# Attention heads taken two at a time: values in both column halves of TensorE's array, scores in both row halves

## Chip, cores and metric

The kernel runs on one core of a Trainium2 chip. The metric is the device time of one execution in microseconds (us). The engines are named as in the profile: PE is TensorE's matmul (PEld its weight loads), DVE is VectorE, ACT is ScalarE, POOL is GpSimd and SP is SyncE. Each engine runs its own queue strictly in order.

## What is computed

256 tokens of width 1024, in float32, pass through two blocks. The first has an HGRN2 mixer, a MoBA attention and a mixture of experts. The second has two layers of FFN, hybrid mixer and FFN. Three attentions matter here. All have 256 queries and 256 keys, so a head's scores are two rows of blocks of 128: 128 queries against 128 keys, and 128 queries against 256 keys.

```python
# MoBA, 8 heads of width 64; one block of 256 keys, so only "own" is left
s_own = einsum('bhqd,bhkd->bhqk', qc, k_own) * scale + rb[:, t5_bucket(dist)]
p = softmax(where(dist >= 0, s_own, -inf));   o = einsum('bhqk,bhkd->bhqd', p, v_own)
# fox, 8 heads of width 64 (in each of two layers)
s_f = einsum('bhqd,bhkd->bhqk', qf, k_f) * scale_f + cf[..., :, None] - cum_f[..., None, :]
p_f = softmax(where(causal, s_f, -inf));      o_f = einsum('bhqk,bhkd->bhqd', p_f, v_f)
# differential, 4 heads with 2 components c of width 64, values of width 128 (two layers)
s_d = einsum('bhcqd,bhckd->bhcqk', qd, k_d) * scale_d
p_d = softmax(where(causal, s_d, -inf));      a_d = p_d[:, :, 0] - lam * p_d[:, :, 1]
o_d = einsum('bhqk,bhkd->bhqd', a_d, v_d)     # then an RMS norm over each head
```

## The kernel before

The whole program is written out by hand: one Python program records the instructions, and the order in which it records them is the order of every engine's queue. No scheduler reorders anything.

**Projections carry the time.** `feat_block` and `tok_block` multiply the 256 tokens by 512 columns of a weight. Numbers are split into a high and a low part, so each product is three matmuls (`mm3`, L295 to L297). After every chunk of 128 rows of the weight the projection calls `fd.tick()`: that is 12 matmuls of 256 columns or 6 of 512. The weights come as raw float32 through a stream of SBUF slots; the **feeder** makes their parts, for 1024 columns at a time (two ticks' worth): ACT copies the high part (L140, buffer `whi`), DVE subtracts to get the low part (L154, `wlo`). `Feeder.fill` issues L140 at the end of every second chunk, just ahead of the tick; the tick runs one step of each background generator and then flushes the waiting L154. So the order on ACT and DVE is: L140 | this tick's step | L154.

**Attention runs in the background.** `moba`, `diff` and `fox` are generators in `fd.bg`; each `yield` ends one tick's step. A head passes through these parts in different ticks: `score` (the matmuls, then on DVE the biased minimum of each block of rows, which also moves the scores out of PSUM, then on ACT the exponential with its sum), `norm` or, in diff, `combine` (DVE: reciprocals, one component minus `lam` times the other), `trans` (three transposes on PE, copied out by ACT as `PT`), and `pv` (values). In `diff` the counter `i` runs over 15 ticks: the score of one component in each of the first 8; `do(3, combine)`, `do(4, trans)`, `do(6, pv)` and `do(8, square)` serve head h at i = first + 2h. After its ticks come the normalisation of the output (`od`, L1706) and, one per tick, two readouts `dx` (four transposes each, copied out by ACT L1717 and DVE L1718). `fox` begins when the diff scores are done and stops after three scores until diff has set `state["diff"]`. `put_heads` (L1782) is the foreground's readout of a projection, four DVE instructions.

**Score operands before.** A head's width is 64, half of the array's 128 rows. Queries of two heads (components) lie one above the other in 128 partitions. The keys, `kp` in MoBA and `kd` in diff, lie in a buffer for each head with the other 64 rows zero, written at the start by `pool.memset`; a score multiplies all 128 rows. fox has padded keys and queries, since two rows of it carry the forget gates.

**Values before.** `pv` of MoBA and fox writes one head's 64 rows of output: its weights are 64 columns wide and use one column half of the array (the trace shows 128*64 as the tile's shape). It does this for one head in a tick.

**PSUM.** Eight banks: four (`pg`) for projections, two (`po`) for the attention's outputs, and two (`pa`) that go round among all the attention's scores (`ms`, `ds`, `fs`), transposes (`mt`, `t3`; the trace calls the latter `t`) and readouts (`dx`). An instruction that takes a `pa` bank waits until the one before in that bank has been read out.

Of the kernel before, what the change touches and what calls it, by code (L numbers as in the profile page):

```python
# [10 lines left out]
F32 = mybir.dt.float32  # L11
# [6 lines left out]
ALU = mybir.AluOpType  # L18
# [162 lines left out]
def body(tc, A, out, taps=None, stop=None):  # L181
# [3 lines left out]
    with es:  # L185
# [12 lines left out]
        def pa(name="a"):  # L198
            return psum.tile([128, 512], F32, tag="a", name=name, bufs=2)
# [258 lines left out]
        def h4(a):  # L458
            return a.rearrange("p (h t) -> p h t", h=4)

        seg = s4[:, 1536:2048]
        pool.memset(seg, 1.0)
# [7 lines left out]
        vm = s6[:, 1024:2048].rearrange("p (t n) -> p t n", t=2)  # L470
        kp = s7.rearrange("p (h s) -> p h s", h=8)
        pool.memset(s7, 0.0)

# [159 lines left out]
        def moba():  # L633
            yield from until("vm")
            Ps, PTk = {}, {}

            def score(h):
                c = h // 2
                s = pa("ms")
                mm(s[:, 0:128], qm[:, c, 0:128], kp[:, h, 0:128], start=True, stop=True)  # L640
                mm(s[:, 128:384], qm[:, c, 128:256], kp[:, h, :], start=True, stop=True)
                P = Pb[h % 4]
                mx = sm(8, "mx")
                dve.tensor_tensor_reduce(P[:, 0:128], s[:, 0:128], TB[:, h, 128:256], 1.0, 3e38, ALU.add, ALU.min,
                                         mx[:, 2:3])
                dve.tensor_tensor_reduce(P[:, 128:384], s[:, 128:384], TB[:, h, :], 1.0, 3e38, ALU.add, ALU.min,
                                         mx[:, 3:4])
                act(P[:, 0:128], P[:, 0:128], AF.Exp, bias=mx[:, 2:3], scale=-1.0, accum_out=mx[:, 4:5])
                act(P[:, 128:384], P[:, 128:384], AF.Exp, bias=mx[:, 3:4], scale=-1.0, accum_out=mx[:, 5:6])
                Ps[h] = P, mx  # L650

# [14 lines left out]

            def pv(h):
                PT = PTk.pop(h)
                c, e = divmod(h, 2)
                o = oT[c // 2][64 * e:64 * e + 64, (c % 2) * 256:(c % 2) * 256 + 256]  # L670
                mm(o, vm[:, 0, h * 64:h * 64 + 64], PT[:, 0:256], start=c % 2 == 0, stop=False, skip_group_check=True)
                mm(o[:, 128:256], vm[:, 1, h * 64:h * 64 + 64], PT[:, 256:384], start=False, stop=c % 2 == 1,
                   skip_group_check=True)

            for i in range(8 + 4):
                if i == 4:
                    oT = [po("mo") for _ in range(2)]
                if i >= 4:
                    pv(i - 4)
                if 2 <= i < 10:  # L680
                    trans(i - 2)
                if 1 <= i < 9:
                    norm(i - 1)
# [31 lines left out]
        for c in range(4):  # L715
            z = halfbank(banks, c)
            act(kp[0:64, 2 * c], z[0:64], AF.Identity, bias=bcol[0:64, 20 + c:21 + c])
            act(kp[64:128, 2 * c + 1], z[64:128], AF.Identity, bias=bcol[64:128, 20 + c:21 + c])
        banks = tok_block()
# [814 lines left out]
        def mixer(l, g_next):  # L1534
            s_qf, s_kf, s_kd, s_d, s_f, s_p = [st.take() for _ in range(6)]
            qf = s_qf.rearrange("p (h t) -> p h t", h=8)
            kf = s_kf.rearrange("p (h t) -> p h t", h=8)
            kd = s_kd.rearrange("p (h t) -> p h t", h=8)
            qd = s_d[:, 0:1024].rearrange("p (h t) -> p h t", h=4)
# [13 lines left out]
            for a in (OH, OL):  # L1553
                pool.memset(a[:, 0:4].bitcast(F32), 0.0)
            for a in (s_kd, s_qf, s_kf):
                pool.memset(a, 0.0)
# [67 lines left out]
            def put_k(b, x2, r2):  # L1624
                for c in range(2):
                    pr_ = slice(64 * c, 64 * c + 64)
                    dve.tensor_tensor(kd[pr_, 4 * b + c:4 * b + 4:2], x2[pr_], r2[pr_], ALU.add)

# [3 lines left out]
            def trans3(P, i):  # L1632
                p = pa("t3")
                for j in range(3):
                    nc.tensor.transpose(p[:, j * 128:(j + 1) * 128], P[:, j * 128:(j + 1) * 128], ident)  # L1635
                PT = PTs[i % 2] if i >= 0 else work.tile([128, 384], F32, name="PT")
                act(PT, p[:, 0:384], AF.Copy)
                return PT

            def diff():  # L1640
# [3 lines left out]

                def score(n):
                    h, c = divmod(n, 2)
                    s = pa("ds")
                    mm(s[:, 0:128], qd[:, h, 0:128], kd[:, n, 0:128], start=True, stop=True)
                    mm(s[:, 128:384], qd[:, h, 128:256], kd[:, n, :], start=True, stop=True)
                    P = PD[n % 5]  # L1650
                    if c == 0:
                        mxs[h] = sm(16, "md")
                    mx = mxs[h]
                    soft(s, P, mx[:, 2 * c:], mx[:, 8 + 2 * c:])
                    Ps[n] = P

# [32 lines left out]
                def trans(h):  # L1689
                    PTk[h] = trans3(Ps[2 * h], h)  # L1690


                for i in range(15):
                    do(6, pv)
                    do(4, trans)
                    do(3, combine)
                    do(8, square)
                    if i < 8:
                        score(i)
                    if i == 7:  # L1700
                        state["diff scores"] = True
                    yield
# [20 lines left out]
            def fox():  # L1723
# [17 lines left out]

                def pv(h):
                    PT = PTk.pop(h)
                    c, e_ = divmod(h, 2)
                    o = oT[c // 2][64 * e_:64 * e_ + 64, (c % 2) * 256:(c % 2) * 256 + 256]
                    mm(o, vf[:, 0, h * 64:h * 64 + 64], PT[:, 0:256], start=c % 2 == 0, stop=False,  # L1746
                       skip_group_check=True)
                    mm(o[:, 128:256], vf[:, 1, h * 64:h * 64 + 64], PT[:, 256:384], start=False, stop=c % 2 == 1,
                       skip_group_check=True)

                def out_(b):
# [4 lines left out]
                while i < 8 + 4:  # L1756
                    if i >= 3 and not {"diff", "vf"} <= state.keys():
                        yield
                        continue
                    if i >= 4:  # L1760
                        oT = oT or [po("fo") for _ in range(2)]
                        pv(i - 4)
# [164 lines left out]
```

## Time and profile before

| | us |
|---|---|
| three runs | 1678.40, 1681.79, 1682.06 (median 1681.79) |
| profiled execution, its own time | 1678.18 |
| its span, first to last instruction | 1676.4 |
| mean granted clock of TensorE | 0.975 of full speed |
| busy: PE / DVE / ACT | 1544.8 / 813.4 / 650.2 |

MoBA stands at about 110 to 143 us, the differential heads and fox of the first layer at about 919 to 983 us; the second layer repeats them later. The times in the rows are the profiler's, counted from the span's start. A busy time of one instruction holds its fill and drain, so successive instructions of one engine overlap in the rows; what one costs in a queue is read from start to start.

### The profile page before, as it was taken

The page shows a single profiled execution, that of the slowest core. Times are in us where ns is not written, and L with a number is a line of the kernel's source. Part 1 is how long each engine was busy: PE and PEld are TensorE (multiplying, and loading weights), DVE is VectorE, ACT ScalarE, POOL GpSimd, SP SyncE. Part 2 cuts the span into 40 slices and gives each one's busy share as a digit, 9 for nine tenths or more (in the row PEclk, how much of TensorE's full clock was granted, in tenths as well). Part 3 has the DMA queues.
Part 4 walks back from the last instruction along what each step waited for, and adds up shares of the span by engine and source line. Part 5 has one row for each costly group of instructions (what it writes and reads, how often), then busy time and mean ns, then how long its engine had stood idle before and what let it go on. Part 6 is the DMA issues. An engine that isn't in the chain of part 4 may idle for free.

```text
span 1676.4 us, 24622 instructions
## 1 busy us (share of the span) xinstructions
PE 1544.8 (92%) x10204; PEld 1209.8 (72%) x10204; DVE 813.4 (49%) x1215; ACT 650.2 (39%) x964; POOL 99.8 (6%) x144
## 2 busy tenths in 40 slices
PE   8999997877687776899999999999999999999998
PEld 7889972222122221699989879999999989889997
DVE  5875650000000000855567866555655568665554
ACT  6456420000000100644445654444544455654442
POOL 4010020000000100100002000000000030000000
PEclk9999999989998898999999999999999999999999
DMA  9657679999999999875614545555555524465510
GB/s 351 172 182 284 259 300 422 421 421 421 421 421 421 419 421 392 350 270 179 198 38 160 215 193 201 197 189 193 189 199 186 169 65 151 176 254 186 194 58 26
DMA packets 85989, 417.53 MB, mean 249 GB/s; under 512 B 7432, under 2 KB 7640, under 8 KB 50544
## 3 DMA queue, kind: packets, MB, share of 16 engines
q1 hardware_dynamic: 82688, 407.07, 64.1%
q0 software_dynamic: 2912, 7.79, 1.6%
q8 instruction: 82, 1.34, 0.3%
q10 hardware_dynamic: 272, 1.05, 0.2%
q14 instruction: 35, 0.29, 0.0%
HBM read 414.60 MB, written 1.25 MB: 248 GB/s over the span
## 4 chain that ended last, share of the span: by engine, by line
PE 56%; DVE 4%; ACT 1%; issue 0%; POOLq 0%; DVEq 0%; POOL 0%; ACTq 0%
PE g L297 9%; PE g L296 8%; PE g L295 8%; PE o L297 5%; PE o L295 5%; PE o L296 5%; PE a L296 3%; PE a L295 3%; PE a L297 3%; DVE wlo L154 1%; PE tp L1368 1%; PE ey L1105 0%; PE fo L1746 0%; PE t L1635 0%; DVE slot L1782 0%
## 5 line engine op out<-in xcount | busy, mean ns | idle before, releaser
L154 DVE TENSOR_TENSOR wlo<-slot,whi 128x1024 fp32r<-128x1024 f32 x268 | 323.3, 1223 | 196.7 <-ACT whi L140 196.5
L140 ACT ACTIVATE whi<-slot 128x1024 fp32r<-128x1024 f32 x268 | 278.3, 1057 | 217.3 <-PE o L296 67.6
L295 PE MATMUL o<-XH,whi 128*128 128x256 f32 x640 | 177.5, 277 | 0.0
L296 PE MATMUL o<-XL,whi 128*128 128x256 f32 x640 | 177.2, 277 | 0.0
L297 PE MATMUL o<-XH,wlo 128*128 128x256 f32 x640 | 177.2, 277 | 0.0
L295 PE MATMUL g<-whi,OH 128*128 128x512 f32 x416 | 165.5, 398 | 0.0
L297 PE MATMUL g<-whi,OL 128*128 128x512 f32 x416 | 164.0, 394 | 0.0
L296 PE MATMUL g<-wlo,OH 128*128 128x512 f32 x416 | 163.1, 392 | 0.0
L295 PE MATMUL a<-XH,whi 128*128 128x256 f32 x512 | 141.8, 277 | 0.0
L296 PE MATMUL a<-XL,whi 128*128 128x256 f32 x512 | 141.7, 277 | 0.0
L297 PE MATMUL a<-XH,wlo 128*128 128x256 f32 x512 | 141.6, 277 | 0.0
L1087 DVE TENSOR_TENSOR eb<-eb,eu 128x512 f32<-128x512 f32 x8 | 5.5, 687 | 265.5 <-PE eu L1083 255.8
L296 PEld LDWEIGHTS o<-XL,whi 128*128 128x128 f32 x640 | 120.4, 188 | 0.7
L295 PEld LDWEIGHTS o<-XH,whi 128*128 128x128 f32 x640 | 120.2, 188 | 0.7
L297 PEld LDWEIGHTS o<-XH,wlo 128*128 128x128 f32 x640 | 120.2, 188 | 0.0
L295 PE MATMUL g<-XH,whi 128*128 128x256 f32 x384 | 114.2, 297 | 0.0
L296 PE MATMUL g<-XL,whi 128*128 128x256 f32 x384 | 107.0, 279 | 0.0
L297 PE MATMUL g<-XH,wlo 128*128 128x256 f32 x384 | 107.0, 279 | 0.0
L1086 ACT ACTIVATE eb<-eg 128x512 f32<-128x512 f32 x8 | 4.8, 597 | 241.7 <-PE eu L1083 191.8
L296 PEld LDWEIGHTS a<-XL,whi 128*128 128x128 f32 x512 | 96.2, 188 | 0.7
L295 PEld LDWEIGHTS a<-XH,whi 128*128 128x128 f32 x512 | 96.1, 188 | 0.7
L297 PEld LDWEIGHTS a<-XH,wlo 128*128 128x128 f32 x512 | 96.2, 188 | 0.0
(531 smaller groups left out, 3486.8 us busy)
## 6 DMA issues: line engine op xcount, KB each, us to landing
slot<-in_gu_dram SPq DMA_DIRECT2D x71, 1024.0 KB, 4.9
slot<-in_w_gate_up_dram SPq DMA_DIRECT2D x46, 1024.0 KB, 19.8
slot<-in_w_in_dram SPq DMA_DIRECT2D x35, 1024.0 KB, 5.1
slot<-in_dn_dram SPq DMA_DIRECT2D x35, 1024.0 KB, 4.9
ew<-in_w_gate_up_dram SPq DMA_DIRECT2D x31, 1024.0 KB, 19.8
slot<-in_w_down_dram SPq DMA_DIRECT2D x29, 1024.0 KB, 19.8
e<-in_w_gate_up_dram SPq DMA_DIRECT2D x15, 1024.0 KB, 19.8
ew<-in_w_down_dram SPq DMA_DIRECT2D x14, 1024.0 KB, 19.8
```

The costliest lines, as they stand in the source:

```text
L140: self.nc.scalar.activation(hi[:, c], src[:, c], AF.Copy)
L154: self.low.tensor_tensor(lo[:, c], src[:, c], hi.bitcast(F32)[:, c], ALU.subtract)
L295: mm(o, sh, mh, start=start, stop=False, skip_group_check=skip)
L296: mm(o, sh, ml, start=False, stop=False, skip_group_check=skip)
L297: mm(o, sl, mh, start=False, stop=stop, skip_group_check=skip)
L1086: act(esg, g, AF.Silu)
L1087: dve.tensor_tensor(esg, esg, u, ALU.mult)
L1368: nc.tensor.transpose(p[:, i * 128:(i + 1) * 128], src[:, c], ident)
```

## The change

Three things are done.

1. **Values in pairs.** A new helper `weighted` takes the values of two heads together, with the instructions of the two alternating; the even head's output goes to rows 0 to 63, the odd one's to 64 to 127. MoBA uses it in odd ticks. fox uses it in odd ticks from i = 5; fox's scores stay as they were. `trans3` gets four buffers in turn for that.
2. **Scores in pairs, without padding.** In MoBA and diff the keys of two heads (components) lie one above the other as the queries do (`km` and `kd`, half as large). `score` takes both: 64 rows of the array each, alternating, into two `pa` banks. Two memsets go, MoBA's eight key copies on ACT become four, and `put_k` is one DVE instruction instead of two. The minima and exponentials of the pair follow in the same tick.
3. **The ticks are dealt out anew.** MoBA still takes 12: scores in even ticks, all else in odd ones. diff takes 14 instead of 15: combine and score in even ticks, square, transposes and values in odd ones.

```diff
+        def weighted(oT, c, v, PT):
+            bank, c0 = oT[c // 2], (c % 2) * 256
+            for t, q, p in ((0, slice(c0, c0 + 256), slice(0, 256)), (1, slice(c0 + 128, c0 + 256), slice(256, 384))):
+                for e, r in enumerate(halves_):
+                    h = 2 * c + e
+                    mm(bank[r, q], v[:, t, h * 64:h * 64 + 64], PT[e][:, p], start=c % 2 == 0 and t == 0,
+                       stop=c % 2 == 1 and t == 1, skip_group_check=True)
...
-            for i in range(8 + 4):
...
+            for i in range(12):
+                c = i // 2
+                if i % 2 == 0:
+                    if c < 4:
+                        score(c)
+                else:
...
+                    if c >= 2:
+                        pv(c - 2)
+                    for e in range(2):
+                        if 1 <= c < 5:
+                            trans(2 * c - 2 + e)
+                    for e in range(2):
+                        if c < 4:
+                            norm(2 * c + e)
...
-                def score(n):
-                    h, c = divmod(n, 2)
-                    s = pa("ds")
-                    mm(s[:, 0:128], qd[:, h, 0:128], kd[:, n, 0:128], start=True, stop=True)
-                    mm(s[:, 128:384], qd[:, h, 128:256], kd[:, n, :], start=True, stop=True)
...
+                def score(h):
+                    ss = [pa("ds") for _ in range(2)]
+                    for q, k, o_ in ((slice(0, 128), slice(0, 128), slice(0, 128)),
+                                     (slice(128, 256), slice(0, 256), slice(128, 384))):
+                        for c, r in enumerate(halves_):
+                            mm(ss[c][:, o_], qd[r, h, q], kd[r, h, k], start=True, stop=True)
+                    mx = mxs[h] = sm(16, "md")
+                    for c, s in enumerate(ss):
+                        P = Ps[2 * h + c] = PD[(2 * h + c) % 5]
+                        soft(s, P, mx[:, 2 * c:], mx[:, 8 + 2 * c:])
...
-                for i in range(15):
-                    do(6, pv)
-                    do(4, trans)
-                    do(3, combine)
-                    do(8, square)
-                    if i < 8:
-                        score(i)
+                for i in range(14):
+                    do(5, pv)
+                    do(3, trans)
+                    do(2, combine)
+                    do(7, square)
+                    do(0, score)
...
-                    if i >= 4:
+                    if i >= 5 and i % 2:
                         oT = oT or [po("fo") for _ in range(2)]
-                        pv(i - 4)
+                        weighted(oT, (i - 5) // 2, vf, [PTk.pop(i - 5 + e) for e in range(2)])
                     if 2 <= i < 10:
-                        PTk[i - 2] = trans3(Ps[i - 2][0], -1)
+                        PTk[i - 2] = trans3(Ps[i - 2][0], i - 2)
```

What this does to the queues is seen in three places. The names are the program's, with buffer numbers: `ds_6119` is a PSUM bank with scores, `md_6099` the small buffer of one head's minima and sums (6099 is head 0 before, 6094 after; 6142 is head 1 in both). `ISA` of L1529 and L1530 (L1541 and L1542 after) are the two minima of a component, each with a row that stores its result.

VectorE in the first layer's diff, before: from the second component's minima of head 0 to the first head's combine (L1659).

```order
L1529 ISA slot6_74,md_6099<-ds_6119,slot0_68 128x128
L1529 ISA md_6099 128x1
L1530 ISA slot6_74,md_6099<-ds_6119,slot0_68 128x256
L1530 ISA md_6099 128x1
L154 TENSOR_TENSOR wlo_6117<-slot3_71,whi_6116 128x1024
L1529 ISA slot6_74,md_6142<-ds_6139,slot0_68 128x128
L1529 ISA md_6142 128x1
L1530 ISA slot6_74,md_6142<-ds_6139,slot0_68 128x256
L1530 ISA md_6142 128x1
L1659 RECIPROCAL md_6099<-md_6099 128x4
```

The same place after.

```order
L1541 ISA slot6_74,md_6094<-ds_6089,slot0_68 128x128
L1541 ISA md_6094 128x1
L1542 ISA slot6_74,md_6094<-ds_6089,slot0_68 128x256
L1542 ISA md_6094 128x1
L154 TENSOR_TENSOR wlo_6116<-slot3_71,whi_6115 128x1024
L1669 RECIPROCAL md_6094<-md_6094 128x4
L1672 TENSOR_SCALAR slot6_74<-slot6_74,md_6094,lam_2230 128x128
L1672 TENSOR_SCALAR slot6_74<-slot6_74,md_6094,lam_2230 128x256
L1675 SCALAR_TENSOR_TENSOR slot6_74<-slot6_74,md_6094 128x128
L1675 SCALAR_TENSOR_TENSOR slot6_74<-slot6_74,md_6094 128x256
L1541 ISA slot6_74,md_6142<-ds_6136,slot0_68 128x128
```

Before, the next head's first minima stood between L154 and the combine of the head before; now they stand behind both.

ScalarE at the same place, before: the exponentials (L1531, L1532) of head 0's two components and of the first component of head 1.

```order
L1531 ACTIVATE slot6_74,md_6099<-slot6_74,md_6099 128x128
L1532 ACTIVATE slot6_74,md_6099<-slot6_74,md_6099 128x256
L140 ACTIVATE whi_6116<-slot3_71 128x1024
L1531 ACTIVATE slot6_74,md_6099<-slot6_74,md_6099 128x128
L1532 ACTIVATE slot6_74,md_6099<-slot6_74,md_6099 128x256
L1531 ACTIVATE slot6_74,md_6142<-slot6_74,md_6142 128x128
```

And after (L1543 and L1544 are the exponentials).

```order
L1543 ACTIVATE slot6_74,md_6094<-slot6_74,md_6094 128x128
L1544 ACTIVATE slot6_74,md_6094<-slot6_74,md_6094 128x256
L1543 ACTIVATE slot6_74,md_6094<-slot6_74,md_6094 128x128
L1544 ACTIVATE slot6_74,md_6094<-slot6_74,md_6094 128x256
L140 ACTIVATE whi_6115<-slot3_71 128x1024
L1543 ACTIVATE slot6_74,md_6142<-slot6_74,md_6142 128x128
```

The feeder's L140 stood between the two components' exponentials; now it stands behind all four of a head.

TensorE where fox goes on after diff, first layer, before: a chunk of six projection matmuls parts fox's tick from the first readout `dx`.

```order
L1635 MATMUL t3_6449<-cst_78,xn0_3822 128x128 x3
L1730 MATMUL fs_6458<-slot5_73,eXH_1703 128x128
L1731 MATMUL fs_6458<-slot5_73,eXH_1703 128x256
L295 MATMUL g_6378<-whi_6219,XH_3818 128x512
L296 MATMUL g_6378<-wlo_6220,XH_3818 128x512
L297 MATMUL g_6378<-whi_6219,XL_3819 128x512
L295 MATMUL g_6379<-whi_6219,XH_3818 128x512
L296 MATMUL g_6379<-wlo_6220,XH_3818 128x512
L297 MATMUL g_6379<-whi_6219,XL_3819 128x512
L1713 MATMUL dx_6474<-cst_78,slot8_76 128x128 x4
```

After, with the last matmul of the chunk ahead and the first of the chunk behind.

```order
L297 MATMUL g_6376<-whi_6163,XL_3814 128x512
L1722 MATMUL dx_6441<-cst_78,slot8_76 128x128 x4
L1645 MATMUL t3_6448<-cst_78,xn0_3817 128x128 x3
L1739 MATMUL fs_6456<-slot5_73,eXH_1698 128x128
L1740 MATMUL fs_6456<-slot5_73,eXH_1698 128x256
L295 MATMUL g_6375<-whi_6223,XH_3813 128x512
```

The readout `dx`, the transposes of fox's head 0 and the scores of its head 2 now stand in one tick and take three `pa` banks, of which there are two.

## Rows read from the trace of the kernel before

**Rows 1.** Page, busy time by engine, whole program.

```profile
PE 1544.8 (92%) x10204; PEld 1209.8 (72%) x10204; DVE 813.4 (49%) x1215; ACT 650.2 (39%) x964; POOL 99.8 (6%) x144
```

**Rows 2.** Chain of waits, first layer's diff: start us, us, what ran.

```profile
920.69 0.96 ACT whi L140
921.67 1.23 DVE wlo L154
```

**Rows 3.** Stretch table: us, busy (count) of PE, PEld, DVE, ACT, POOL, clock, DMA, GB/s.

```profile
917.50:943.70 26.20, 25.85 (x203) 24.59 (x202) 20.93 (x65) 17.13 (x51) 0.00 (x0) 1.00 0.34 121
```

**Rows 4.** Timeline, PE, one differential tick: start us, us, instruction.

```profile
919.55 0.38 PE L1648 MATMUL ds<-eXL,slot 128*128 128x128 f32 x2
...
921.59 0.38 PE L1648 MATMUL ds<-eXL,slot 128*128 128x128 f32 x2
```

**Rows 5.** Timeline, DVE, differential heads of the first layer.

```profile
919.37 0.28 DVE L1529 CUSTOM_DVE_ANT_0 slot<-ds,slot 128x128 f32<-128x128 f32 x1
...
922.81 0.28 DVE L1529 CUSTOM_DVE_ANT_0 slot<-ds,slot 128x128 f32<-128x128 f32 x1
...
923.37 0.17 DVE L1659 RECIPROCAL md<-md 128x4 f32<-128x4 f32 x1
...
924.82 0.28 DVE L1529 CUSTOM_DVE_ANT_0 slot<-ds,slot 128x128 f32<-128x128 f32 x1
...
926.51 2.79 DVE L1782 SCALAR_TENSOR_TENSOR slot<-g,rsb 64x512 f32<-64x512 f32 x4
...
931.34 0.28 DVE L1529 CUSTOM_DVE_ANT_0 slot<-ds,slot 128x128 f32<-128x128 f32 x1
...
937.53 0.74 DVE L1665 SCALAR_TENSOR_TENSOR slot<-slot,md 128x128 f32<-128x128 f32 x2
```

**Rows 6.** Timeline, ACT, the same stretch.

```profile
919.70 0.40 ACT L1531 ACTIVATE slot<-slot,md 128x128 f32<-128x128 f32 x1 [1.95 <-DVE md L1529]
...
920.59 1.05 ACT L140 ACTIVATE whi<-slot 128x1024 fp32r<-128x1024 f32 x1
```

**Rows 7.** Timeline, PE, a chunk of 12 matmuls, and diff's last transposes.

```profile
938.24 0.28 PE L295 MATMUL g<-XH,whi 128*128 128x256 f32 x1
...
939.60 0.28 PE L295 MATMUL g<-XH,whi 128*128 128x256 f32 x1
...
940.61 0.49 PE L1635 MATMUL t<-cst,slot 128*128 128x128 f32 x3
```

**Rows 8.** Timeline, DVE, end of diff and start of fox.

```profile
949.18 0.16 DVE L1738 RECIPROCAL mx<-mx 128x2 f32<-128x2 f32 x1
...
950.61 0.69 DVE L1706 TENSOR_TENSOR slot<-do,r 128x512 f32<-128x512 f32 x1
```

**Rows 9.** Timeline, ACT, readout of the turned differential output.

```profile
954.37 0.67 ACT L1717 ACTIVATE OH<-dx,wr 128x512 fp32r<-128x512 f32 x1
```

**Rows 10.** Timeline, PE, fox: a tick without values, then one with.

```profile
958.84 0.40 PE L297 MATMUL g<-whi,OL 128*128 128x512 f32 x1
...
961.21 0.40 PE L297 MATMUL g<-whi,OL 128*128 128x512 f32 x1
961.54 0.65 PE L1746 MATMUL fo<-PT,slot 128*64 128x256 f32 x2
...
964.53 0.40 PE L297 MATMUL g<-whi,OL 128*128 128x512 f32 x1
```

**Rows 11.** Timeline, PE, experts' down product in four column tiles.

```profile
360.84 0.62 PE L1105 MATMUL ey<-ew,eb 128*32 128x512 f32 x1
...
360.86 0.62 PE L1105 MATMUL ey<-slot,eb 128*32 128x512 f32 x2
361.30 0.59 PE L1105 MATMUL ey<-ew,eb 128*32 128x512 f32 x1
```

**Rows 12.** Stretch table, two stretches beside the experts' last weights.

```profile
676.80:680.20 3.40, 1.36 (x9) 0.84 (x8) 3.34 (x5) 3.40 (x5) 0.97 (x2) 1.00 1.02 429
680.30:683.60 3.30, 2.90 (x7) 2.11 (x7) 2.88 (x6) 1.81 (x4) 0.09 (x1) 0.50 1.03 432
```

More of the change, by code (lines that the diff above doesn't have):

```diff
@@ L635, in moba, with score @@
             Ps, PTk = {}, {}
[L637 to L650, printed above, removed]
+            def score(c):
+                ss = [pa("ms") for _ in range(2)]
+                for q, k, o in ((slice(0, 128), slice(0, 128), slice(0, 128)),
+                                (slice(128, 256), slice(0, 256), slice(128, 384))):
+                    for e, r in enumerate(halves_):
+                        mm(ss[e][:, o], qm[r, c, q], km[r, c, k], start=True, stop=True)
+                for e, s in enumerate(ss):
+                    h = 2 * c + e
+                    P = Pb[h % 4]
+                    mx = sm(8, "mx")
+                    dve.tensor_tensor_reduce(P[:, 0:128], s[:, 0:128], TB[:, h, 128:256], 1.0, 3e38, ALU.add, ALU.min,
+                                             mx[:, 2:3])
+                    dve.tensor_tensor_reduce(P[:, 128:384], s[:, 128:384], TB[:, h, :], 1.0, 3e38, ALU.add, ALU.min,
+                                             mx[:, 3:4])
+                    act(P[:, 0:128], P[:, 0:128], AF.Exp, bias=mx[:, 2:3], scale=-1.0, accum_out=mx[:, 4:5])
+                    act(P[:, 128:384], P[:, 128:384], AF.Exp, bias=mx[:, 3:4], scale=-1.0, accum_out=mx[:, 5:6])
+                    Ps[h] = P, mx
             def norm(h):
@@ L665, in trans, with pv @@
                 PTk[h] = PT
[L667 to L673, printed above, removed]
-            for i in range(8 + 4):
-                if i == 4:
-                    oT = [po("mo") for _ in range(2)]
-                if i >= 4:
-                    pv(i - 4)
[L680 to L683, printed above, removed]
-                if i < 8:
-                    score(i)
+            def pv(c):
+                weighted(oT, c, vm, [PTk.pop(2 * c + e) for e in range(2)])
+            for i in range(12):
[4 more added lines that the diff above has]
+                else:
+                    if c == 2:
+                        oT = [po("mo") for _ in range(2)]
+                    if c >= 2:
[6 more added lines that the diff above has]
+                            norm(2 * c + e)
                 if i == 8:
@@ L715, in body @@
         for c in range(4):
[L716 to L718 removed]
+            act(km[:, c], halfbank(banks, c), AF.Identity, bias=bcol[:, 20 + c:21 + c])
         banks = tok_block()
@@ L1554, in mixer @@
                 pool.memset(a[:, 0:4].bitcast(F32), 0.0)
-            for a in (s_kd, s_qf, s_kf):
+            for a in (s_qf, s_kf):
                 pool.memset(a, 0.0)
@@ L1624, in put_k @@
             def put_k(b, x2, r2):
-                for c in range(2):
-                    pr_ = slice(64 * c, 64 * c + 64)
-                    dve.tensor_tensor(kd[pr_, 4 * b + c:4 * b + 4:2], x2[pr_], r2[pr_], ALU.add)
+                dve.tensor_tensor(kd[:, 2 * b:2 * b + 2], x2, r2, ALU.add)
             def put_q(b, x2, r2):
@@ L1635, in trans3 @@
                     nc.tensor.transpose(p[:, j * 128:(j + 1) * 128], P[:, j * 128:(j + 1) * 128], ident)
-                PT = PTs[i % 2] if i >= 0 else work.tile([128, 384], F32, name="PT")
+                PT = PTs[i % 4] if i % 4 < 2 else work.tile([128, 384], F32, name="PT")
                 act(PT, p[:, 0:384], AF.Copy)
```

27 lines of the change are left out of this document (5 added, 22 removed).

## Prediction

> **What bounds the kernel now.** I read the page first: PE is busy 1544.8 us, DVE 813.4, ACT 650.2 [rows 1]. On that average anything that shortens PE's queue shortens the kernel. An average hides the stage, so I then read the stretch that the change touches. In the first layer's differential heads PE is still filled, but DVE has 20.93 us of work in a stretch of 26.20, ACT 17.13 [rows 3], and the chain of waits of that stretch steps from ACT's L140 to DVE's L154 rather than along PE [rows 2]. The reader is to see that PE is saturated there with some 20% to spare on DVE, and that this spare holds only while DVE's order stays good: whatever puts DVE's and ACT's steps one behind the other becomes the bound. So the amounts of work that the change saves on PE are one question, and the order on DVE and ACT the other.
>
> **The prices.** A tick with the score of one differential component takes 921.59 − 919.55 = 2.04 us on PE [rows 4], a projection chunk alone 939.60 − 938.24 = 1.36 [rows 7]; one component's score costs PE 0.68. A fox tick with values takes 964.53 − 961.21 = 3.32, one without 961.21 − 958.84 = 2.37 [rows 10]; one head's values cost 0.95, more than their columns need, since PE enters and leaves the half-array shape each time. On DVE a component's minima cost 923.37 − 922.81 = 0.56, L154 922.81 − 921.67 = 1.14 [rows 2, 5], combine 924.82 − 923.37 = 1.45, put_heads 2.79 [rows 5]. On ACT a component's exponentials cost 920.59 − 919.70 = 0.89, and they begin 919.70 − 919.37 = 0.33 after their minima; L140 costs 1.05 [rows 5, 6].
>
> **Values in pairs.** Two heads side by side in the two column halves are not in this trace. The nearest rows are the experts' down product: four column tiles start within 0.02 us, and the next four follow 0.46 later, the length of one and not of four [rows 11]. So I take a pair at the price of one head, 0.95. The other end is no overlap, 2 × 0.95 less one change of shape. One head's values have as many columns as a component's score (0.68), so I estimate the change of shape at 0.95 − 0.68 = 0.27, and this end at 2 × 0.68 + 0.27 = 1.6 a pair. MoBA: 8 × 0.95 − 4 × 0.95 = 3.8 saved. Fox the same, less 0.3 for one change of shape that its last heads, with little between them, share already: 3.5 saved a layer.
>
> **Scores in pairs.** Row halves side by side are not in this trace either. If they run side by side, a pair costs 0.68 plus a change of shape, 0.95, instead of 1.36; if not, 1.63. Between the ends I take the first, by the same rows 11 (tiles that do not touch run together). MoBA has no cover for PE there, so four pairs save 4 × 0.41 = 1.6 (other end: they cost 1.1). MoBA's DVE and ACT steps grow no longer in a chain, as L140 stands ahead of its exponentials; I add no wait. The dropped memsets (POOL) and the four fewer copies on ACT save nothing on the path: POOL is busy 99.8 us of the whole program [rows 1], and the copies end a tick or more before the scores. **MoBA together: −5.4.**
>
> **Diff: the new order on DVE and ACT.** Here the scores' price hardly matters, because PE will wait. Follow one pair in the new order. Both components' minima are on DVE; 0.33 after the first, ACT begins four exponentials (2 × 0.89 = 1.79); only then comes L140 (1.05), because it stands behind all four; behind it DVE's L154 (1.14); behind that the combine (1.45), which had been ready since the exponentials; and behind the combine the next pair's minima. That is a ring: 0.33 + 1.79 + 1.05 + 1.14 + 1.45 = **5.76 us a pair**. PE's own need for a pair is two chunks 2.72, scores 0.95, values 0.68 and transposes 0.34 (estimates from the score: as many columns, and half as many): 4.7. Before, L140 slipped in between a head's exponentials, and the steady beat of DVE was 931.34 − 924.82 − 2.79 = 3.73 a pair [rows 5]: PE was the bound.
>
> I walk the ring from the first minima, which stand where they stood, 919.37: second pair 925.13, third 930.89 and 2.79 for put_heads makes 933.68, fourth 939.44, last combine done 945.20. Before, it was done at 937.53 + 0.74 = 938.27 [rows 5], and the last transposes stood at 940.61, PE's own pace [rows 7]. Now they follow the combine at about 945.3: +4.7. They also stand one tick earlier in the projection, so one chunk more, 1.36, lies behind them: **+6.1 a layer.** The other ends: if the ring didn't hold, PE would set the pace and diff would gain 4 × 0.41 = 1.6 instead; if row halves did not overlap, the ring covers their 0.68 a pair.
>
> The Trainium skill speaks for and against this change. Its page TensorEngine Tiling (Array Packing) gives in the section Theoretical Speedup up to twofold for a dimension of 64 or less; its section PSUM Bottleneck says that "Tiling speeds up TensorE but not PSUM evacuation". The first alone would give the first rival's time below, the second points where my forecast goes; the trace of before agrees with the second as far as it can, with DVE's 20.93 us of 26.20.
>
> **Start of fox.** One tick now holds the readout dx0, fox's transposes and its third score, three takers of two banks. The transposes wait for fox's second minima, which stand on DVE behind a norm and the two output normalisations. From the norm's first instruction to the first normalisation pass 950.61 − 949.18 = 1.43, in which one head's minima (0.56) run too, so a norm is 0.87; with 2 × 0.69 it makes 2.25 [rows 8]. dx0 itself, two thirds of a score's columns, covers 0.45: 1.8. The third score waits until dx0 is read out by L1717 (0.67), which stands on ACT behind two exponentials and L140: 0.89 + 1.05 + 0.67 = 2.6 [rows 6, 9]. So 1.8 + 2.6 = **+4.4 a layer**; what little this place loses now I leave out. Other end: zero, if ACT and DVE get there early enough.
>
> **The sum.** A layer: 6.1 + 4.4 − 3.5 = +7.0. Two layers +14.0, MoBA −5.4, net **+8.6**. What hides it? Around both mixers PE is the bound (DMA is busy 0.34 of the diff stretch [rows 3]), so a delay there passes through to the end. The profiled execution took 1678.18 around a span of 1676.4: 1686.8 on its basis. The runs shown are 1678.4, 1681.79 and 1682.06; on their median, 3.6 above the profiled one, it is 1690.4. With four executions, two at 1678.3 and two at 1681.9, I take 1680 as the basis: **1688.6**.
>
> **Rivals.**
> (a) *The ring doesn't close; PE stays the bound.* This ends on the faster side. It decides at a beat on DVE of 4.7 us a pair: below it PE never waits. For it: DVE's 3.73 now, and the page's 813.4 against 1544.8. Against it: the order of the queues, in which L140 has no way past the exponentials. The time: MoBA −5.4, a layer −3.5 − 1.6 and no cost at the start of fox: −15.6, 1664.4. It is also the time of the skill's page by speedup alone.
> (b) *The ring holds, but the start of fox costs nothing.* The stall in diff lets ACT and DVE empty their queues before fox goes on. Then a layer is 6.1 − 3.5 = +2.6, two +5.2, less 5.4: 1679.8, no change. For it: DVE idles when PE waits. Against: dx0 needs its readout whatever came before.
> (c) *The halves do not run side by side*, so the change doesn't do what it says. Values cost 1.6 a pair: 12 pairs × 0.65 = +7.8, and MoBA's scores +2.7; diff's are covered. 1680 + 8.6 + 10.5 = 1699.1. Against it: rows 11.
> (d) *The clock falls in the new gaps.* At the end of the first block the granted clock was 1.00 of 2.4 GHz while PE had 1.36 us of work in 3.40, and 0.50 in the next 3.30 us [rows 12]: half speed for one such stretch costs 1.7. The gaps here reach 2.6 us, twice a layer, with work between. Two falls: +3.3, 1691.9.
>
> **Chances.** Forecast 0.58, (a) 0.08, (b) 0.16, (c) 0.07, (d) 0.11. The forecast's own range is 1684 to 1692 (terms uncertain by a third). The range for 8 in 10 takes in (b) and (d) and most of the way to (c): 1679 to 1697; (a), (c) and the tails are left out. A difference of 0.2%, 3.4 us, is about what a measurement of this kernel can tell. Faster by more: (a) and a little of (b), 0.11. Within: most of (b) and the low edge of the forecast, 0.16. Slower: 0.73.
>
> **What would show it.** In the changed kernel's timeline of DVE, first minima of successive differential heads 5.8 apart (8.5 where put_heads stands between), L154 directly ahead of each combine, and the last transposes 4.7 later than now; a beat of 4.7 or less refutes the ring. In PE's rows, a wait of about 1 us a pair in diff released by DVE, and two of 2 to 3 us where fox goes on. Values: rows of the two halves starting within 0.05 us of each other; starts 0.2 apart would show (c). MoBA's last values 5 us earlier. A granted clock under 1.00 in the diff stretch would show (d). The forecast is wrong if PE's waits in a mixer sum to less than 5 us.

## The result, and the profile after

The changed kernel takes 1692.49 us (median of four runs, 1689.18 to 1695.11) against 1680.53 before; the ratio is 1.0067, 95% interval 1.0053 to 1.0080. So it is slower by 11 to 12 us. The forecast was 1688.6, in a range of 1679 to 1697.

The profiled execution took 1689.18 us. Its page, busy time by engine, beside [rows 1]:

```profile
PE 1538.8 (91%) x10204; PEld 1203.3 (71%) x10204; DVE 808.7 (48%) x1211; ACT 645.8 (38%) x960; POOL 94.5 (6%) x141
```

PE's own work fell by 6 us and the span grew by 11 (1676.4 to 1687.4). The time went into waits, and into matmuls at half the clock behind some of them. The waits of PE in the first layer's mixer (engine, line, what it waited for: us in total, times, longest), before and then after:

```profile
PE t L1635 <- DVE slot L1665: 0.2, 1, 0.2
```

```profile
PE t L1645 <- DVE md L1542: 4.0, 2, 2.1
PE fs L1739 <- ACT slot L1647: 2.0, 1, 2.0
PE t L1645 <- DVE mx L1542: 1.8, 1, 1.8
PE t L1645 <- DVE slot L1675: 0.6, 1, 0.6
PE ds L1661 <- ACT slot L1647: 0.5, 1, 0.5
```

Before there was next to nothing; after, 8.9 us. The first, fourth and fifth row lie in diff, the second and third where fox goes on. The second layer has the same five, of the same sizes.

**The ring in diff.** DVE of the changed kernel, first layer, beside [rows 5] (start us, us, instruction):

```profile
912.67 0.28 DVE L1541 CUSTOM_DVE_ANT_0 slot<-ds,slot 128x128 f32<-128x128 f32 x1
...
915.84 1.23 DVE L154 TENSOR_TENSOR wlo<-slot,whi 128x1024 fp32r<-128x1024 f32 x1 [1.98 <-ACT whi L140]
916.98 0.17 DVE L1669 RECIPROCAL md<-md 128x4 f32<-128x4 f32 x1
...
918.43 0.28 DVE L1541 CUSTOM_DVE_ANT_0 slot<-ds,slot 128x128 f32<-128x128 f32 x1
...
922.75 2.79 DVE L1782 SCALAR_TENSOR_TENSOR slot<-g,rsb 64x512 f32<-64x512 f32 x4
...
927.12 0.29 DVE L1541 CUSTOM_DVE_ANT_0 slot<-ds,slot 128x128 f32<-128x128 f32 x1
...
932.89 0.28 DVE L1541 CUSTOM_DVE_ANT_0 slot<-ds,slot 128x128 f32<-128x128 f32 x1
...
938.00 0.74 DVE L1675 SCALAR_TENSOR_TENSOR slot<-slot,md 128x128 f32<-128x128 f32 x2
```

and ACT, from a pair's first exponential to L140:

```profile
913.00 0.40 ACT L1543 ACTIVATE slot<-slot,md 128x128 f32<-128x128 f32 x1 [1.95 <-DVE md L1541]
...
914.28 0.49 ACT L1544 ACTIVATE slot<-slot,md 128x256 f32<-128x256 f32 x1
...
914.77 1.04 ACT L140 ACTIVATE whi<-slot 128x1024 fp32r<-128x1024 f32 x1
```

The first minima of the four heads stand at 912.67, 918.43, 927.12 and 932.89. A step without `put_heads` (L1782) is 5.76 us, as forecast; the one with it is 8.69. Each of the four L154 waits 1.98 us for ACT's L140, which begins when the fourth exponential ends. The combine (L1669) stands right behind L154, or behind `put_heads` where that comes between. From the first minima to the end of the last combine are 938.74 − 912.67 = 26.07 us; before they were 938.27 − 919.37 = 18.90 [rows 5].

**The start of fox.** PE, from the last transposes of diff to the first readout and fox's head 2:

```profile
938.40 0.83 PE L1645 MATMUL t<-cst,slot 128*128 128x128 f32 x3 [0.58 <-DVE slot L1675]
...
949.42 0.66 PE L1722 MATMUL dx<-cst,slot 128*128 128x128 f32 x4
951.90 0.55 PE L1645 MATMUL t<-cst,xn 128*128 128x128 f32 x3 [1.82 <-DVE mx L1542]
954.47 0.80 PE L1739 MATMUL fs<-slot,eXH 128*128 128x128 f32 x2 [2.02 <-ACT slot L1647]
```

The two waits of the forecast, 1.8 and 2.6, are there with 1.82 and 2.02. The third score itself takes longer than in [rows 4], and the stretch table tells why (us, busy and count of PE, PEld, DVE, ACT, POOL, clock, DMA, GB/s):

```profile
919.00:921.00 2.00, 1.87 (x11) 1.87 (x12) 0.63 (x6) 2.00 (x9) 0.00 (x0) 0.69 0.00 0
921.00:923.00 2.00, 2.00 (x12) 1.72 (x12) 1.40 (x2) 0.94 (x2) 0.00 (x0) 0.50 0.00 0
953.00:954.00 1.00, 0.00 (x0) 0.00 (x0) 0.00 (x0) 1.00 (x3) 0.00 (x0) 0.94 0.26 98
954.00:957.20 3.20, 2.73 (x8) 2.26 (x8) 2.41 (x9) 1.13 (x5) 0.00 (x0) 0.50 0.00 0
957.50:959.00 1.50, 1.50 (x10) 1.27 (x9) 0.44 (x1) 0.41 (x1) 0.00 (x0) 1.00 0.19 22
```

The two long waits of PE in the ring:

```profile
919.13 0.55 PE L1645 MATMUL t<-cst,slot 128*128 128x128 f32 x3 [1.93 <-DVE md L1542]
...
927.82 0.55 PE L1645 MATMUL t<-cst,slot 128*128 128x128 f32 x3 [2.10 <-DVE md L1542]
```

The granted clock fell to 0.50 of 2.4 GHz, the 1.2 GHz level, twice in this layer, each time after PE had waited: behind the wait that ends at 919.13, and during the second of the two at the start of fox (0.94 in the stretch up to 954.00, in which PE stood still). Not every such wait was followed by a fall: behind the one that ends at 927.82 the clock stayed at 1.00. The second layer shows the same two falls. The first lies in the ring, which kept its beat through it (8.69 against 0.33 + 1.79 + 1.05 + 1.14 + 2.79 + 1.45 = 8.55 by the prices). Behind the second PE has no more waits: 3.2 us at half speed cost it some 1.6.

**The tiles.** PE at the first pair of differential scores, and in fox from a pair of values to the same place two ticks on:

```profile
914.70 0.93 PE L1661 MATMUL ds<-eXL,slot 64*128 64x128 f32 x8
915.56 0.39 PE L295 MATMUL g<-XH,whi 128*128 128x256 f32 x1
915.78 0.28 PE L296 MATMUL g<-XL,whi 128*128 128x256 f32 x1
```

```profile
968.74 0.87 PE L469 MATMUL fo<-slot,slot 128*64 128x256 f32 x8
969.54 0.55 PE L1645 MATMUL t<-cst,xn 128*128 128x128 f32 x3
...
975.24 0.55 PE L1645 MATMUL t<-cst,xn 128*128 128x128 f32 x3
```

Eight row-half matmuls and the return to the full shape take 915.78 − 914.70 less one projection matmul (0.11, a twelfth of the chunk in [rows 7]): 0.97, where 0.95 was forecast and two full scores cost 1.36. Two fox ticks with one pair of values take 975.24 − 969.54 = 5.70, before 2 × 3.32 = 6.64 [rows 10]; a pair saves 0.94, as forecast. In both, the two matmuls of a couple start less than 0.01 us apart. Both kinds of tiles run side by side.

**MoBA.** DVE's last readout of MoBA's output, before and after:

```profile
147.02 1.29 DVE L301 TENSOR_TENSOR OB<-mo,OB 128x512 fp32r<-128x512 f32 x2 [1.59 <-ACT OB L300]
```

```profile
141.32 1.29 DVE L301 TENSOR_TENSOR OB<-mo,OB 128x512 fp32r<-128x512 f32 x2 [0.74 <-ACT OB L300]
```

It comes 5.7 us earlier; 5.4 was forecast.

**The cost by stage.** The projections' matmuls (L295 to L297) are the same 7488 in every kernel, in the same order, so one and the same matmul can be found in two traces. Between the starts of the same two of them each stage takes longer (+) or shorter than before by (us; the times are those of MoBA and of the first layer):

| stage | before, from and to | after, from and to | first layer | second layer | forecast |
|---|---|---|---|---|---|
| MoBA | 106.19, 144.33 | 106.17, 138.44 | −5.9 (once) | | −5.4 |
| diff | 904.52, 946.21 | 897.81, 945.70 | +6.2 | +6.2 | +6.1 |
| start of fox | 946.21, 956.32 | 945.70, 961.15 | +5.3 | +5.4 | +4.4 |
| rest of fox (values) | 956.32, 984.74 | 961.15, 986.74 | −2.8 | −2.8 | −3.5 |

Without rounding that is +8.70 and +8.82 for the two mixers and −5.86 for MoBA, +11.7 together. Kernels whose edits leave a stage alone agree with before there within 0.1 us, so this comparison tells far smaller differences than the times do.

### The profile page after: what moved, and what is told of

It is laid out like the page before. It is cut to its first block, busy times and chain, and to the rows that moved or that the text cites. A ratio compares the mean times of both kernels' runs of the same rounds, so it can differ in the third digit from the quotient of the medians.

```text
span 1687.4 us, 24602 instructions
## 1 busy us (share of the span) xinstructions
PE 1538.8 (91%) x10204; PEld 1203.3 (71%) x10204; DVE 808.7 (48%) x1211; ACT 645.8 (38%) x960; POOL 94.5 (6%) x141
## 3 DMA queue, kind: packets, MB, share of 16 engines
q10 hardware_dynamic: 272, 1.05, 0.2%
## 4 chain that ended last, share of the span: by engine, by line
PE 65%; DMA 25%; DVE 5%; ACT 3%; issue 1%; POOL 1%; SPq 0%; POOLq 0%; DVEq 0%; ACTq 0%
PE g L295 11%; PE g L297 11%; PE g L296 11%; DMA ew<-in_w_gate_up_dram 6%; DMA slot<-in_w_down_dram 6%; DMA slot<-in_w_gate_up_dram 6%; PE o L297 5%; PE o L295 5%; PE o L296 5%; PE a L295 4%; PE a L296 4%; PE a L297 4%; DMA e<-in_w_gate_up_dram 2%; DMA eOB<-in_w_gate_up_dram 1%; DMA m<-in_w_gate_up_dram 1%; DMA ew<-in_w_down_dram 1%
## 5 line engine op out<-in xcount | busy, mean ns | idle before, releaser
L154 DVE TENSOR_TENSOR wlo<-slot,whi 128x1024 fp32r<-128x1024 f32 x268 | 323.4, 1223 | 216.7 <-ACT whi L140 216.5
L140 ACT ACTIVATE whi<-slot 128x1024 fp32r<-128x1024 f32 x268 | 278.2, 1056 | 222.3 <-PE a L296 66.3
L295 PE MATMUL o<-XH,whi 128*128 128x256 f32 x640 | 177.2, 277 | 0.0
L297 PE MATMUL o<-XH,wlo 128*128 128x256 f32 x640 | 176.9, 276 | 0.0
L295 PE MATMUL g<-whi,OH 128*128 128x512 f32 x416 | 165.3, 397 | 0.0
L297 PE MATMUL g<-whi,OL 128*128 128x512 f32 x416 | 163.9, 394 | 0.0
L295 PE MATMUL a<-XH,whi 128*128 128x256 f32 x512 | 141.5, 276 | 0.0
L297 PE MATMUL a<-XH,wlo 128*128 128x256 f32 x512 | 141.4, 276 | 0.0
L295 PEld LDWEIGHTS o<-XH,whi 128*128 128x128 f32 x640 | 120.1, 188 | 0.7
L297 PEld LDWEIGHTS o<-XH,wlo 128*128 128x128 f32 x640 | 120.2, 188 | 0.0
L295 PE MATMUL g<-XH,whi 128*128 128x256 f32 x384 | 112.9, 294 | 0.0
L297 PE MATMUL g<-XH,wlo 128*128 128x256 f32 x384 | 107.7, 281 | 0.0
L295 PEld LDWEIGHTS a<-XH,whi 128*128 128x128 f32 x512 | 96.1, 188 | 0.7
L297 PEld LDWEIGHTS a<-XH,wlo 128*128 128x128 f32 x512 | 96.1, 188 | 0.0
```

The lines of the kernel that those rows point to most:

```text
L140: self.nc.scalar.activation(hi[:, c], src[:, c], AF.Copy)
L154: self.low.tensor_tensor(lo[:, c], src[:, c], hi.bitcast(F32)[:, c], ALU.subtract)
L295: mm(o, sh, mh, start=start, stop=False, skip_group_check=skip)
L297: mm(o, sl, mh, start=False, stop=stop, skip_group_check=skip)
```

## Experiments

Times are medians, set against the kernel before in runs on the same chip (1680.6 for the three single parts and for the kernel that opens the ring, 1681.1 for the last one, 1681.2 for the others). An interval reaches 2 to 4 us to either side, so differences of that size between two kernels are not settled by the times alone. Where they matter, the traces are compared as in the table above, between the same two matmuls.

### The parts apart

MoBA's part alone (`score`, `pv`, the loop and `km` of the change):

```diff
-        kp = s7.rearrange("p (h s) -> p h s", h=8)
-        pool.memset(s7, 0.0)
+        km = s7[:, 0:1024].rearrange("p (c t) -> p c t", c=4)
...
-            def score(h):
+            def score(c):
...
+                        mm(ss[e][:, o], qm[r, c, q], km[r, c, k], start=True, stop=True)
...
+                weighted(oT, c, vm, [PTk.pop(2 * c + e) for e in range(2)])
```

> Only MoBA's part of the change (scores and values in pairs); diff and fox as before. Theory (the loss sits in the two mixers of the second block, in diff's order on ACT and DVE and where fox goes on; MoBA gains): 5.4 to 6.7 us faster than before, 1674 to 1675. Rival (paired tiles cost time wherever they stand): no gain, 1680 or more.

Measured: 1674.16, ratio 0.9965 [0.9951, 0.9979], −6.4 us, as the theory has it; between the same matmuls MoBA's stage is 5.9 us shorter.

fox's values alone:

```diff
-                    if i >= 4:
-                        pv(i - 4)
+                    if i >= 5 and i % 2:
+                        weighted(oT, (i - 5) // 2, vf, [PTk.pop(i - 5 + e) for e in range(2)])
```

> Only fox's values in pairs; MoBA, diff and all scores as before. Theory: 3.5 us a layer, 7 us faster than before, 1673. Rival (a pair of value tiles waits for the second head's transposes, so the gain goes into a wait): 0 to 2 us faster.

Measured: 1674.69, ratio 0.9968 [0.9958, 0.9978], −5.9 us: 3.0 a layer instead of 3.5, and 2.8 between the same matmuls. PE shows no new wait there, so the rival falls.

diff's part alone:

```diff
-                def score(n):
+                def score(h):
...
+                            mm(ss[c][:, o_], qd[r, h, q], kd[r, h, k], start=True, stop=True)
...
-                for i in range(15):
+                for i in range(14):
```

> Only diff's part (scores in pairs without padding, 14 ticks); MoBA and fox's values as before. Theory: the whole loss of the change is here: 11.3 measured for all, plus some 6 for MoBA and 7 for fox's values that are missing: 24 to 25 us slower than before, 1704 to 1706. Rival (the parts disturb each other): under 15 us slower.

Measured: 1708.22, ratio 1.0169 [1.0152, 1.0186], +27.6 us, somewhat over the range. The whole loss of the change is in this part. By the times the three parts sum to −6.4 − 5.9 + 27.6 = +15.3, against 11 to 12 for the change as a whole. Between the same matmuls they do add up: −5.9 for MoBA, −5.5 for fox's values in two layers and +23.4 for diff's part make +12.0, and the whole change has +11.7. What is left over, −0.7 to +1.4 us in each of the four profiled executions, lies in stretches that no edit touches.

MoBA's part and fox's values together, diff as before. The edit is the first two of these diffs in one kernel; of diff's own lines this one stays:

```diff
                 for i in range(15):
                     do(6, pv)
```

> MoBA's part and fox's value pairs together, diff as before. Theory (these two add up, and the change's diff part is all loss): -6.4 and -5.9 as measured apart, 1668 to 1669, as fast as the change with one tick of delay (1668.4), so that pairing diff's scores brings nothing even when its order is mended. Rival (pairing diff's scores brings its PE time, some 2 us a layer, once the order is mended): 1672 or more.

Measured: 1667.74, ratio 0.9924 [0.9899, 0.9948], −13.5 us. The two gains add up: without its diff part the change makes the kernel faster.

### Opening the ring

One empty tick ahead of diff's loop moves its parity against the feeder's:

```diff
+                yield
                 for i in range(14):
                     do(5, pv)
```

> The changed kernel with one more empty tick ahead of diff's loop, nothing else: now the feeder's L140 stands ahead of a pair's four exponentials instead of behind them, and the first readout dx0 is a tick apart from fox's transposes. Theory (the ring minima, exponentials, L140, L154, combine, and the crowded tick at fox's start make the loss): the beat of a pair falls from 5.8 to PE's own 4.7 to 5.0, and the time is MoBA -6, a layer -3.5 -1.6 +0.2: 1663 to 1667, faster than before and than the change. Rival (two components in one tick cost by themselves, through both PSUM banks taken at once): the beat stays at 5.5 or more and the time at 1685 or more.

Measured: 1668.42, ratio 0.9925 [0.9909, 0.9942], −12.2 us, 24 us less than the changed kernel for one line. ACT of this kernel, first layer: the load of its function table ahead of the first pair's exponentials, then the last exponential of that pair, L140, and the first exponential of the next pair:

```profile
915.97 1.28 ACT L1543 ACT_TABLE_LOAD   x1
...
918.54 0.49 ACT L1544 ACTIVATE slot<-slot,md 128x256 f32<-128x256 f32 x1
...
919.03 1.04 ACT L140 ACTIVATE whi<-slot 128x1024 fp32r<-128x1024 f32 x1
920.95 0.40 ACT L1543 ACTIVATE slot<-slot,md 128x128 f32<-128x128 f32 x1 [0.87 <-DVE md L1541]
```

and DVE's first minima of the four heads, with the first combine:

```profile
915.81 0.29 DVE L1541 CUSTOM_DVE_ANT_0 slot<-ds,slot 128x128 f32<-128x128 f32 x1 [0.52 <-PE ds L1661]
...
919.16 0.18 DVE L1669 RECIPROCAL md<-md 128x4 f32<-128x4 f32 x1 [1.02 <-ACT slot L1544]
...
920.62 0.29 DVE L1541 CUSTOM_DVE_ANT_0 slot<-ds,slot 128x128 f32<-128x128 f32 x1
...
927.26 0.29 DVE L1541 CUSTOM_DVE_ANT_0 slot<-ds,slot 128x128 f32<-128x128 f32 x1
...
930.96 0.29 DVE L1541 CUSTOM_DVE_ANT_0 slot<-ds,slot 128x128 f32<-128x128 f32 x1
```

DVE's queue has the same order as in the changed kernel. What differs is which L140 an L154 waits for: the one issued ahead of the pair's exponentials, no longer the one behind them. The beats are 4.81 and 3.70, and 6.64 with `put_heads`: the ring's 5.76 is gone. They don't measure PE's own pace, for which 4.7 was forecast: in the first, the combine waits 1.02 us for exponentials that the table load held up, and in the last, behind `put_heads`, DVE catches up. What is left of waits on PE:

```profile
PE t L1645 <- DVE md L1542: 1.7, 2, 1.5
```

1.5 of these 1.7 us stand at the pair with `put_heads`, whose 2.79 us DVE can't hide within one beat. The time is 1 to 5 us over the expectation, and level with the kernel that leaves diff alone (1667.74) as far as their intervals tell, 3 to 4 us. The traces tell more: between the same matmuls diff takes 0.4 and 0.2 us longer than before in the two layers of this kernel, and 0.0 in those of the kernel that leaves it alone. So pairing diff's scores gains nothing even in the better order.

### The start of fox by itself

The changed kernel with the ring left as it is, and one empty tick behind diff's loop:

```diff
                     yield
+                yield
                 st.give(s_kd, s_d)
```

> The changed kernel with one empty tick after diff's loop: the readouts dx come one tick later, apart from fox's transposes and third score, while the order inside diff (L140 behind a pair's exponentials) stays. Theory (ring and start of fox are two costs): the ring's beat of 5.8 stays, the two waits at fox's start (1.8 and 2.0) go, and with them the fall of the clock behind them: 4.4 + 1.7 us a layer, 1679 to 1684. Rival (the crowded tick only shows a delay that the ring has made): 1689 or more, the waits move elsewhere.

Measured: 1680.57, ratio 0.9999 [0.9988, 1.0011]. The first minima still follow each other at 5.77:

```profile
915.72 0.28 DVE L1541 CUSTOM_DVE_ANT_0 slot<-ds,slot 128x128 f32<-128x128 f32 x1
...
921.49 0.28 DVE L1541 CUSTOM_DVE_ANT_0 slot<-ds,slot 128x128 f32<-128x128 f32 x1
```

but PE's waits of the layer are now only those in diff:

```profile
PE t L1645 <- DVE md L1542: 4.6, 2, 2.7
PE ds L1661 <- ACT slot L1647: 0.5, 1, 0.5
```

The two waits at the start of fox are gone, and with them the second fall of the clock. Against the before of their own runs the two kernels stand at −0.6 and +12.0, so by the times the crowded tick costs 6.3 us a layer. Between the same matmuls it is 5.3 and 5.4, and this is accounted for: waits of 1.8 and 2.0, and 1.6 for the clock behind them. In diff both kernels take 6.2 us a layer longer than before. The ring costs what lies between this kernel and the one with the tick ahead of the loop: −0.6 against −12.2, 5.8 us a layer by the times, 5.8 and 6.0 between the same matmuls.

The reverse, the ring open and the tick crowded again (fox begins one tick later):

```diff
                 yield from until_("diff scores")
-                yield from wait(1)
+                yield from wait(2)
...
+                yield
                 for i in range(14):
```

> The changed kernel with the empty tick ahead of diff's loop (ring open, 1668.4), and fox begun one tick later, so that dx0, fox's transposes and its third score meet in one tick again. Theory: the crowded tick costs by itself, 4.4 us a layer, and up to 1.7 more if the clock falls: 1676 to 1681. Rival (without the ring's backlog ACT and DVE read out in time): 1670 or less.

Measured: 1673.77, ratio 0.9955 [0.9942, 0.9969], 5.3 us slower than with the tick apart (1668.42). PE's waits in the first layer, and the stretch behind the last of them:

```profile
PE t L1645 <- DVE md L1542: 1.7, 2, 1.6
PE t L1645 <- DVE mx L1542: 1.1, 1, 1.1
PE fs L1740 <- ACT slot L1647: 1.1, 1, 1.1
```

```profile
948.00:951.50 3.50, 3.37 (x10) 2.81 (x11) 1.75 (x8) 1.06 (x5) 0.00 (x0) 0.55 0.84 286
```

The crowded tick makes its waits and its fall of the clock without the ring too, but the waits are 1.1 and 1.1, not 1.8 and 2.0: ACT and DVE have less queued up when fox goes on. The time lies between the two expectations: that the tick costs by itself is shown (3.4 and 3.9 us a layer between the same matmuls), its full price of 5.3 and 5.4 needs the ring's backlog.

### What the row halves are worth

The kernel with the ring open, but diff's keys zero-padded again, a pair of scores as two full matmuls:

```diff
-                            mm(ss[c][:, o_], qd[r, h, q], kd[r, h, k], start=True, stop=True)
+                            mm(ss[c][:, o_], qd[:, h, q], kd[:, 2 * h + c, k], start=True, stop=True)
```

> The changed kernel with the empty tick ahead of diff's loop, but diff's keys in the old form with zero padding, so that a pair of scores runs as two full matmuls of 128 rows one behind the other instead of side by side in the row halves; order and ticks the same. Theory (in diff the wait for DVE covers part of PE): row halves save 0.5 us a pair on PE, of which at most half arrives: 0 to 2 us slower than 1668.4 for two layers. Rival (PE sets the pace there): 8 pairs x 0.5 = 4 us slower, 1672.5.

Measured: 1670.41, ratio 0.9940 [0.9921, 0.9959], −10.8 us where the kernel with row halves has −12.2; the intervals of the two overlap. PE waits 1.2 us for DVE here and 1.7 there, so part of what the halves save is waited away. Between the same matmuls the mixers take 0.1 and 0.4 us longer than with row halves: 0.5 us for two layers, within the theory's 0 to 2, and the rival's 4 us falls.

The same in MoBA, on the kernel that has MoBA's part alone:

```diff
-                        mm(ss[e][:, o], qm[r, c, q], km[r, c, k], start=True, stop=True)
+                        mm(ss[e][:, o], qm[:, c, q], kp[:, 2 * c + e, k], start=True, stop=True)
```

> Only MoBA's part, and of it the pairs, ticks and value halves as changed, but the keys in the old form with zero padding: a pair of scores is two full matmuls of 128 rows one behind the other. Theory (PE sets MoBA's pace, so row halves count there): four pairs cost 0.5 us more each, 2 us slower than MoBA's whole part (1674.2), 1676. Rival (MoBA's gain of 6.4 comes from its waits and value halves alone): 1674 to 1675.

Measured: 1675.01, ratio 0.9964 [0.9953, 0.9975], 0.9 us slower than MoBA's part with row halves; by the time alone this settles nothing. In the traces, MoBA's first minima and the last readout of its output, first with row halves (MoBA's part alone) and then padded:

```profile
113.10 0.28 DVE L658 CUSTOM_DVE_ANT_0 m<-ms,slot 128x128 f32<-128x128 f32 x1
...
141.55 1.29 DVE L301 TENSOR_TENSOR OB<-mo,OB 128x512 fp32r<-128x512 f32 x2 [0.74 <-ACT OB L300]
```

```profile
114.48 0.28 DVE L659 CUSTOM_DVE_ANT_0 m<-ms,slot 128x128 f32<-128x128 f32 x1
...
143.58 1.29 DVE L301 TENSOR_TENSOR OB<-mo,OB 128x512 fp32r<-128x512 f32 x2 [0.75 <-ACT OB L300]
```

The padded kernel's readout comes 2.03 us later, but 1.38 of that it has lost before MoBA began (114.48 against 113.10), in a start in which the granted clock of this execution was 0.50 from 17.2 to 20.2 us, and 1.00 in the other. So the row halves are worth 0.65 us for four pairs, not the theory's 2; between the same matmuls it is the same 0.6 (−5.9 against −5.2). PE's own work falls by more, some 1.2 us. The rest goes into a wait that the padded kernel doesn't have:

```profile
PE mt L676 <- DVE mx L660: 0.5, 1, 0.5
```

The rival is nearer: most of MoBA's gain, 5.2 of 5.9, comes without the row halves.

## Why the prediction was right

**The bound, and the ring (+6.1 a layer).** Right, in mechanism and size. The prices of [rows 2, 5, 6] chained in the new queues' order gave 5.76 us a pair, and the trace has 5.76. Diff took 6.2 us a layer longer than before, and opening the ring gave 5.8 to 6.0 of it back. The 3.73 that I called DVE's steady beat before is no more than its own work for a pair (2 × 0.56 + 1.14 + 1.45 = 3.71), done without a pause behind `put_heads`; that PE was the bound before holds all the same. The last transposes were put 4.7 us later, measured from the first minima; 938.40 − 912.67 is 25.73, before 940.61 − 919.37 = 21.24, so 4.5.

**The start of fox (+4.4 a layer).** The mechanism was right, the term too small: 5.3 and 5.4 between the same matmuls (6.3 by the times). Its waits were a little over-priced (1.8 and 2.6; measured 1.82 and 2.02). What was missing is the fall of the clock behind them, which the forecast held apart as rival (d) with a chance of 0.11. The two are not rivals: the waits that the forecast counted on are what the clock fell after. With (d)'s two falls the sum would have been 1691.9, close to what was measured; so (d) was right beside the forecast. Its sign came too, a clock under 1.00 in the diff stretch, but that fall is hidden by the ring; the one that cost time stands at the start of fox.

**fox's values (−3.5 a layer).** Right in mechanism, over by 0.7: 2.8 between the same matmuls (3.0 by the time of the part alone). The three pairs that stand between other steps save 0.94 each, 2.8 together; so the last pair, whose heads already stood together before, saves next to nothing, where I had taken off 0.3 only.

**MoBA (−5.4).** −5.9 between the same matmuls, −6.4 in the time of the part alone. That the sum came out is in part luck, for its two terms are off in opposite ways. Row halves were to save 1.6 and saved 0.65: a part of what PE saved went into a wait, where I had added none. Values and new ticks were to save 3.8 and saved 5.2, and here a wait of PE for DVE fell away (0.8 us before, none in the padded kernel). That tiles which do not touch run together, as taken from [rows 11], held for both kinds.

**The rivals.** (a), PE stays the bound, fell with the beat of 5.76; the kernel with one more tick shows what (a) would have been, and it is 1668.4 rather than 1664.4, since pairing diff's scores brings nothing and fox's values bring less than forecast. (b), a free start of fox, fell with the waits there. (c) fell with the tiles.

**The sum (+8.6).** The stages measured +11.7. The 3.1 between come from the start of fox (2.0 for two layers), fox's values (1.4) and diff (0.2), less 0.5 for MoBA.

**The reading of the scores.** The Trainium skill, TensorEngine Tiling (Array Packing), section PSUM Bottleneck, says that tiling speeds up TensorE but not the evacuation of PSUM. The trace agrees in direction: PE's work fell by 6 us, and DVE's and ACT's reading of the scores, with the feeder's steps between, set the pace in diff. But the evacuation was no slower than before: DVE's work as a whole fell (808.7 us against 813.4), and one empty tick took the loss away. The order of the queues lost the time.

**What stays open.** Whether the pairs in diff are worth anything once DVE has room for `put_heads`; that wasn't tried. Why a wait of some 2 us of PE in the ring was followed by a lower clock in some places and not in others.

## What to carry to other kernels

When a step is moved to be done in pairs, write down every engine's queue over one period of the new order and add the durations around any closed chain: if the ring is longer than the bound engine's own work, the saving turns into a loss, however idle the other engines look on average. Look first at work of another stream (here the feeder's L140 and L154) that the larger batch now stands ahead of; the remedy may be one tick of phase. And count how many takers of a small ring of banks meet in one step before moving two generators against each other.

## What the runs showed of the hardware

- Column halves (128*64) and row halves (64*128) run side by side: a pair of heads' values saves 0.94 us of PE and a pair of scores takes 0.97 instead of twice 0.68, the change of shape included. What arrives can be less: the row halves were worth 0.65 us for MoBA's four pairs and 0.5 us for diff's eight.
- The granted clock fell to the 1.2 GHz level for some 3.2 us with the second of PE's two waits at the start of fox, wherever there were such waits (waits of 1.8 and 2.0 us, or of 1.1 and 1.1; both layers of three kernels). Of the two waits of 1.9 to 2.7 us in the ring, one in each layer had a fall with it (three kernels); single waits of 1.2 to 1.6 us there had none (the three kernels with the ring open). Where PE is the bound behind it, a fall adds some 1.6 us to the price of the wait. PE was busy for 1.87 to 2.00 of every 2 us, or 2.73 of 3.20, through the slow stretches of the changed kernel.
- A kernel that does less on every engine (PE, DVE, ACT and POOL are each some 4 to 6 us less busy) was 11 to 12 us slower.
